# The normalised input of an encoder layer: rows scaled on VectorE and transposed plainly, in place of products with a diagonal

## The chip, the core and the metric

The kernel runs on one core of a Trainium2 chip. Its time is device microseconds of one execution. TensorE does the matmuls and transposes (PE in the rows, PEld is its loading of weights), VectorE (DVE) and ScalarE (ACT) the elementwise work, GpSimd (POOL) small things, and SyncE (SP) issues most transfers.

## The reference

One layer of a hybrid encoder on 256 tokens of width 2048, all in f32: a feed-forward part, a mixing part (attention and convolution), and a second feed-forward part. Each part reads a modulated, normalised input, and its result is normalised and added to x:

```python
def rms_norm(x, g):
    y = xf * lax.rsqrt(jnp.mean(xf * xf, axis=-1, keepdims=True) + NORM_EPS)
    return (y * g.astype(jnp.float32)).astype(x.dtype)

def modulate(h, shift, scale):
    return h * (1.0 + scale[:, None, :]) + shift[:, None, :]
...
        mod = c_act @ w_ada[l] + b_ada[l]
        (sh1, sc1, g1, sh2, sc2, g2, sh3, sc3, g3) = jnp.split(mod, N_MOD, axis=-1)
        h = modulate(rms_norm(x, ffn1_pre_g[l]), sh1, sc1)
        f = swiglu(h, ffn1_w_gate[l], ffn1_w_up[l], ffn1_w_down[l])
        x = x + 0.5 * g1[:, None, :] * rms_norm(f, ffn1_post_g[l])
```

The other two parts begin and end in the same way, with their own gains and modulation vectors.

## The kernel before

x stays on chip as two token tiles of 128 tokens by 2048 (t0 and t1). A product needs its input with the width on partitions, so each part's input is made in 16 K tiles of 128 columns, transposed. `pre_norm` does this two K tiles at a time: a matmul of a 128x128 block of x with a diagonal matrix that holds 1/rms of its tokens (`dg`, made by `diag_of`) transposes and scales it into a PSUM tile `pst` (there are two such places), ACT multiplies by A and adds B (`hf`, line 377; A is (1 + scale) times the gain, B the shift), and `split_to` splits the result into two float32r parts: the high part is a cast on ACT (line 360), the low part a subtraction on VectorE (line 361). All weights are split in the same way (`wchunk`: cast on ACT, subtraction on VectorE, lines 286 and 287), and each product is three matmuls, high by high, high by low and low by high (lines 312 to 314; the moving operand is 512 columns of the weight). The block products with `dg` are plain f32.

`pre_norm` is called at six places. (1) At the start, for K tiles 0 to 3. (2) In the first feed-forward, whose first round of products goes through the 16 K tiles in four stages of four: while the products of a stage run, VectorE sums up the modulation vectors of the next one from transferred pieces of `w_ada` (`mod_sum`, line 190, advanced a little with each weight chunk), TensorE transposes the sums into columns (line 204), ACT copies those (line 209), and then `pre_norm` makes the next stage's K tiles. (3) At the second boundary, between the first feed-forward and the mixing part, for all 16 K tiles, by `next_norm`: residual of t0 (`post_add`, lines 400 to 408), four K tiles of t0, residual of t1, then the rest. (4) At the third boundary, between mixing and second feed-forward, in the same way for four K tiles. (5, 6) In the two later stages of the second feed-forward, six K tiles each.

1/rms comes from `rstd_parts`: the sum of squares is made by ACT (line 335), scaled on VectorE (at the start on ACT), and raised to the power -0.5 on POOL (line 347, tile `r`). `pr` is the same for the part's result before it is added.

The order on each engine is that of a scheduler that follows the program, and each engine takes its instructions strictly in that order.

Of the kernel before, what the change touches and what calls it, by code (L numbers as in the profile page):

```python
# [36 lines left out]
# Chunks over which token tile 0 runs ahead of tile 1 at a part's start and end, and K tiles of  # L37
# tile 0's input that come before the rest.
# [3 lines left out]
# Steps of background work per weight chunk: convolution, modulation in the first feed-forward  # L42
# and in the mixing part.
# [3 lines left out]
# Chunks between an elementwise result and its transposes: rope, activations, conv input.  # L47
# [3 lines left out]
# Buffers for chunks as loaded, and for each of their two parts.  # L51
# [3 lines left out]
# K tiles of the first products of each feed-forward, by stages of their modulation.  # L55
# [5 lines left out]
def encoder_layer(ctx, tc, a, consts, out):  # L61
# [80 lines left out]
    def load_cols(names, i):  # L142
        """Parameter vectors with element j*128+p at [p, j]."""
        rows = work.tile([P, P], F32, tag="rows", name=f"rows{i}")
        at = 0
        for name in names:
            n = a[name].shape[1] // P
            nc.gpsimd.dma_start(rows[at:at + n, :], a[name].rearrange("o (j p) -> (o j) p", p=P))
            pcols[name] = (at, n, i)
            at += n  # L150
        prm = keep.tile([P, sum(a[n].shape[1] for n in names) // P], F32, name=f"prm{i}")
        ps = tr_ps(f"ps_prm{i}")
        nc.tensor.transpose(ps[:, :at], rows[:at, :], ident[:at, :at])
        nc.scalar.copy(prm[:, :at], ps[:, :at])
        pcols[i] = prm
# [12 lines left out]
    def mod_sum(vs, c0, n):  # L168
        """Partial sums over the partitions of columns c0..c0+n of the vectors vs."""
# [26 lines left out]
    def mod_cols(vs, dsts, c0, n):  # L196
        """Columns c0..c0+n of the vectors vs with element j*128+p at dst[p, j]."""
# [17 lines left out]
    def mod_affine(vsh, vsc, gname, A, B, c0, n):  # L215
        """A = (1 + scale) * pre gain, B = shift, for columns c0..c0+n."""
# [9 lines left out]
    def mod_gate(v, gname, factor, gc):  # L226
        """gc = factor * vector v * post gain."""
# [4 lines left out]
    def gate_tile(gc, i):  # L232
        """The column vector gc as a row, the same on every partition."""
# [11 lines left out]
    def slot(tag, shape, name, dt=F32):  # L245
        """A tile of at most SLOT elements in a place that several parts use in turn."""
# [29 lines left out]
    def wchunk(w, r0, kt, cols, name):  # L276
        """K tiles from row r0 on, of 512 columns in equal parts from each of cols on."""
# [12 lines left out]
    class Group:  # L290
        """ps[t] (+)= x[t] @ w over K tiles k0..k0+nk and 512 columns; xT holds the K tiles
        from kx on."""
# [23 lines left out]
    def in_step(work):  # L316
        """Chunks of groups, all of token tile 0 before token tile 1."""
# [7 lines left out]
    def group(*args, head=0, tail=0, **kw):  # L325
        """A group, token tile 0 ahead of tile 1 over the first head and the last tail chunks."""
# [10 lines left out]
    def rstd_parts(ssp, n, name, act=False):  # L337
        """(sum of the columns of ssp / n + EPS) ** -0.5"""
        k = ssp.shape[-1]
        ms, r = small(f"s_{name}", 1), small(name, 1)  # L340
# [9 lines left out]
    def diag_of(r, name, act=False):  # L350
        d = work.tile([P, P], F32, tag="diag", bufs=2, name=name)
        if act:
            nc.scalar.activation(d, ident, AF.Copy, scale=r)
        else:
            nc.vector.tensor_scalar(d, ident, r, None, op0=ALU.mult)
        return d

# [5 lines left out]
    def pre_norm(hT, dg, A, B, j0, j1, i, t0=0, t1=NT):  # L363
        """K tiles j0..j1 of modulate(rms_norm(x)) transposed, for token tiles t0..t1; dg
        holds 1/rms on diagonals."""
        n = (t1 - t0) * P
        for j in range(j0, j1, 2):
            ps = tr_ps(f"pst{i}_{j}_{t0}")
            hf = work.tile([P, 2, S], F32, tag="hf", bufs=2, name=f"hf{i}_{j}_{t0}")
            h = hf[:, :, :n]  # L370
            for jj in range(2):
                o = ps[:, jj * S:jj * S + n]
                for t in range(t0, t1):
                    nc.tensor.matmul(o[:, (t - t0) * P:(t - t0 + 1) * P],  # L374
                                     x[:, t, (j + jj) * P:(j + jj + 1) * P], dg[t],
                                     start=True, stop=True)
# [4 lines left out]
    def transposed(src, ps, n=2):  # L381
        """[P tokens, t, n*128] -> PSUM [128, n, S]."""
# [17 lines left out]
    def post_add(f, r, i, t):  # L400
        """x += f * r for token tile t, r the rstd of the rows before the gain; returns 1/rms
        of the new rows on a diagonal."""
# [5 lines left out]
        return diag_of(rstd_parts(sx, D, f"r{i}_{t}"), f"dg{i}_{t}")  # L408

    def next_norm(f, ssp, A, B, j1, i):  # L410
        """Residual, and the first j1 K tiles of the next part's input, token tile 0 first over
        the chunks of a group's head."""
        hT = Parts(f"h{i}", "h", range(4))
        jh = min(HEAD * CH, j1)
        dg = [post_add(f, post_rstd(ssp, i, 0), i, 0)]
        pre_norm(hT, dg, A, B, 0, JF, i, 0, 1)
        dg.append(post_add(f, post_rstd(ssp, i, 1), i, 1))
        pre_norm(hT, dg, A, B, JF, jh, i, 0, 1)
        pre_norm(hT, dg, A, B, 0, jh, i, 1, 2)
        pre_norm(hT, dg, A, B, jh, j1, i)  # L420
        return hT, dg

# [43 lines left out]
    def ffn_start(hT, wg, wu, i, stages, mods_of, norm_of, last_lane, begin=None):  # L466
        """Blocks of the first round, K tiles in stages: a stage's modulation is summed up
        while the products of the stage before run."""
# [64 lines left out]
    # ================= first feed-forward =================  # L533
# [29 lines left out]
    dg = [diag_of(rstd_parts(sx[t], D, f"r0_{t}", act=True), f"dg0_{t}", act=True) for t in range(NT)]  # L563
# [3 lines left out]
    pre_norm(hT, dg, A1, B1, *STAGES1[0], "1_0")  # L567

    def begin2(open_group, run, order):
        """The first two groups with token tile 0 ahead."""  # L570
# [10 lines left out]
    def later_mods():  # L581
        yield from mod_gate(2, "ffn1_post_g", 0.5, g1)
        for c0 in range(0, D, MW):
# [4 lines left out]
                   lambda s: pre_norm(hT, dg, A1, B1, *STAGES1[s], f"1_{s}"),  # L588
# [4 lines left out]
    hT, dg = next_norm(f, ssp, A2, B2, NK, 2)  # L593

    # ================= attention and convolution =================
# [42 lines left out]
    def rope_T(pt, name, tag):  # L638
        """PSUM t x [P, 4 heads x 128] -> rotated and transposed [128, head, S]."""
# [26 lines left out]
    def attention(hb, qT, kT):  # L666
        """Heads of one half in overlapping steps: scores, transpose, output."""
# [58 lines left out]
    def attn_parts(hb, hi, lo):  # L726
        """Attention rows times their gain, transposed; 1/rms is applied after the product."""
# [30 lines left out]
    # layer norm over channels, swish: sums over channels on the tensor engine  # L758
# [9 lines left out]
    def rstd_cols(ps, n, name):  # L768
        """Sums of [128 equal rows, S tokens] -> 1/rms with the tokens on partitions."""
# [107 lines left out]
    for db in range(4):  # L877
        po = mm_ps(f"pc{db}")
        group(po, mT, w_out, 8, 8, db * BLK, f"oc{db}", kx=8, tail=TAIL if db == 3 else 0)
        for t in range(NT):  # L880
# [4 lines left out]
    # ================= second feed-forward =================  # L885
    hT, dg = next_norm(f, ssp, A3, B3, STAGES2[0][1], 3)
    aT = ffn_start(hT, a["ffn2_w_gate"], a["ffn2_w_up"], 2, STAGES2, ffn2_mods,
                   lambda s: pre_norm(hT, dg, A3, B3, *STAGES2[s], f"3_{s}"),
# [64 lines left out]
```

## Time and profile before

| | |
|---|---|
| time, median of 3 runs | 2000.48 us (1996.08 to 2004.53) |
| span of the profiled execution | 1997.8 us |
| TensorE busy | 1917.2 us (96%) |
| VectorE busy | 1466.7 us (73%) |
| ACT busy | 936.7 us (47%) |
| POOL busy | 65.5 us (3%) |
| transfers | 493.13 MB, mean 247 GB/s |

A busy share is an average over the whole span. Matmuls overlap on TensorE, so the length of one matmul record is longer than the distance to the next. One f32 block product shows as two records in the trace, one plain transpose as one. In the rows, `out<-in` names the tiles by their names in the program, and what stands in brackets is the idle time of the engine ahead of the instruction and what ended it. The granted clock is a share of TensorE's full 2.4 GHz.

### The profile page before, as it was taken

How to read it: one execution, taken by the hardware profiler on the slowest of the kernel's cores; microseconds unless marked ns; L12 is line 12 of the kernel's file. 1: busy time of each engine (PE TensorE's matmuls, PEld its weight loads, DVE VectorE, ACT ScalarE, POOL GpSimd, SP SyncE). 2: the span in 40 equal slices, each digit the busy share in tenths (PEclk: the TensorE clock that was granted, in tenths of full speed). 3: DMA queues.
4: the chain of work that ended last, by engine and by line, in shares of the span. 5: the costliest groups of instructions: out<-in, count | busy, mean ns of one | idle time of the engine just before them, and what ended most of it. 6: DMA issues, size and time to landing. Idle time of an engine off the chain costs nothing.

```text
span 1997.8 us, 23978 instructions
## 1 busy us (share of the span) xinstructions
PE 1917.2 (96%) x8547; PEld 1552.7 (78%) x8547; DVE 1466.7 (73%) x1780; ACT 936.7 (47%) x1439; POOL 65.5 (3%) x90
## 2 busy tenths in 40 slices
PE   2999999999999999899999997999999999999997
PEld 2888888888888877678888786888888777888886
DVE  6789999777777766589997758898776455444454
ACT  3554455444444444644455745635444433444442
POOL 2000000000000000000100000000000000000000
PEclk9999999999999999899999998999999999999999
DMA  9989988999999977356656667998777667656552
GB/s 341 313 296 307 318 266 280 344 320 327 313 318 322 301 251 262 104 176 184 179 167 203 195 205 243 329 325 278 245 224 234 216 231 236 198 180 186 172 189 96
DMA packets 249432, 493.13 MB, mean 247 GB/s; under 512 B 17065, under 2 KB 42433, under 8 KB 249312
## 3 DMA queue, kind: packets, MB, share of 16 engines
q1 hardware_dynamic: 247888, 491.38, 73.8%
q8 instruction: 67, 1.10, 0.2%
q14 instruction: 53, 0.43, 0.1%
q0 software_dynamic: 1248, 0.15, 0.1%
q10 hardware_dynamic: 176, 0.07, 0.0%
HBM read 489.44 MB, written 2.10 MB: 246 GB/s over the span
## 4 chain that ended last, share of the span: by engine, by line
PE 85%; DMA 7%; DVE 4%; issue 2%; ACT 1%; POOL 0%; DVEq 0%; POOLq 0%; ACTq 0%; SPq 0%
PE pg_t L312 8%; PE pg_t L313 8%; PE pg_t L314 8%; PE pu_t L313 8%; PE pu_t L314 7%; PE pu_t L312 7%; DMA ada<-in_w_ada 7%; PE pd_t L313 6%; PE pd_t L314 6%; PE pd_t L312 6%; PE pc_t L312 2%; PE pc_t L313 2%; PE pc_t L314 2%; PE pst L374 1%; DVE lo_d L287 1%
## 5 line engine op out<-in xcount | busy, mean ns | idle before, releaser
L190 DVE SCALAR_TENSOR_TENSOR acc<-ada,cact,acc 128x512 f32<-128x512 f32 (+2 forms) x448 | 394.2, 900 | 148.4 <-DMA ada<-in_w_ada 138.0
L286 ACT CAST hi_d<-raw_d 128x1024 fp32r<-128x1024 f32 x176 | 184.4, 1050 | 273.6 <-PE pd_t L314 233.8
L286 ACT CAST hi_g<-raw_g 128x1024 fp32r<-128x1024 f32 x176 | 184.8, 1051 | 241.4 <-PE pg_t L314 143.8
L287 DVE TENSOR_TENSOR lo_d<-raw_d,hi_d 128x1024 fp32r<-128x1024 f32 x176 | 212.7, 1223 | 111.1 <-ACT hi_d L286 110.7
L286 ACT CAST hi_u<-raw_u 128x1024 fp32r<-128x1024 f32 x176 | 184.7, 1050 | 219.3 <-PE pu_t L314 121.7
L287 DVE TENSOR_TENSOR lo_u<-raw_u,hi_u 128x1024 fp32r<-128x1024 f32 x176 | 214.3, 1223 | 95.9 <-ACT hi_u L286 95.3
L287 DVE TENSOR_TENSOR lo_g<-raw_g,hi_g 128x1024 fp32r<-128x1024 f32 x176 | 214.4, 1223 | 77.1 <-ACT hi_g L286 76.7
L313 PE MATMUL pd_t<-lo_d,a_0h 128*128 128x512 f32 x384 | 152.3, 397 | 4.3 <-DVE lo_d L287 4.2
L312 PE MATMUL pd_t<-hi_d,a_0h 128*128 128x512 f32 x384 | 152.4, 397 | 0.0
L314 PE MATMUL pd_t<-hi_d,a_0l 128*128 128x512 f32 x384 | 151.7, 395 | 0.0
L312 PE MATMUL pg_t<-hi_g,h3h 128*128 128x512 f32 x352 | 141.2, 401 | 1.8 <-ACT h3h L360 1.8
L312 PE MATMUL pg_t<-hi_g,h1h 128*128 128x512 f32 x352 | 140.5, 400 | 0.2 <-ACT h1h L360 0.2
L312 PE MATMUL pu_t<-hi_u,h1h 128*128 128x512 f32 x352 | 140.4, 399 | 0.0
L312 PE MATMUL pu_t<-hi_u,h3h 128*128 128x512 f32 x352 | 140.2, 398 | 0.0
L313 PE MATMUL pg_t<-lo_g,h1h 128*128 128x512 f32 x352 | 139.8, 397 | 0.0
L313 PE MATMUL pg_t<-lo_g,h3h 128*128 128x512 f32 x352 | 139.8, 397 | 0.0
L314 PE MATMUL pg_t<-hi_g,h3l 128*128 128x512 f32 x352 | 139.8, 397 | 0.0
L314 PE MATMUL pg_t<-hi_g,h1l 128*128 128x512 f32 x352 | 139.7, 397 | 0.0
L313 PE MATMUL pu_t<-lo_u,h1h 128*128 128x512 f32 x352 | 139.7, 397 | 0.0
L313 PE MATMUL pu_t<-lo_u,h3h 128*128 128x512 f32 x352 | 139.4, 396 | 0.3 <-DVE lo_u L287 0.3
L314 PE MATMUL pu_t<-hi_u,h3l 128*128 128x512 f32 x352 | 139.4, 396 | 0.0
L314 PE MATMUL pu_t<-hi_u,h1l 128*128 128x512 f32 x352 | 139.2, 396 | 0.0
(258 smaller groups left out, 3631.3 us busy)
## 6 DMA issues: line engine op xcount, KB each, us to landing
ada<-in_w_ada SPq DMA_DIRECT2D x288, 512.0 KB, 5.4
raw_g<-in_ffn_w_gate SPq DMA_DIRECT2D x176, 512.0 KB, 4.9
raw_u<-in_ffn_w_up SPq DMA_DIRECT2D x176, 512.0 KB, 4.9
raw_d<-in_ffn_w_down SPq DMA_DIRECT2D x176, 512.0 KB, 5.3
raw_c<-in_w_in SPq DMA_DIRECT2D x64, 256.0 KB, 3.0
raw_q<-in_w_in SPq DMA_DIRECT2D x16, 512.0 KB, 3.7
raw_k<-in_w_in SPq DMA_DIRECT2D x16, 512.0 KB, 3.7
raw_v<-in_w_in SPq DMA_DIRECT2D x16, 512.0 KB, 3.6
```

The source lines that it names most:

```text
L190: nc.vector.scalar_tensor_tensor(acc, w[:, j, :], cact[:, j0 + j:j0 + j + 1], acc, op0=ALU.mult, op1=ALU.add)
L286: nc.scalar.copy(h, r)
L287: nc.vector.tensor_tensor(l, r, f32(h), op=ALU.subtract)
L312: nc.tensor.matmul(o, xh, h, start=self.first and k == 0, stop=False)
L313: nc.tensor.matmul(o, xh, l, start=False, stop=False)
L314: nc.tensor.matmul(o, xl, h, start=False, stop=self.last and k == self.nk - 1)
L374: nc.tensor.matmul(o[:, (t - t0) * P:(t - t0 + 1) * P], x[:, t, (j + jj) * P:(j + jj + 1) * P], dg[t], start=True, stop=True)
```

## The change

The diagonal goes away. 1/rms itself is kept (`rx`). For each pair of K tiles and each token tile, VectorE writes x times 1/rms into a new tile `xn` of 128x256 (three places), and TensorE transposes its two halves with the identity matrix, as plain transposes. ACT's conversions, the splits and all else stay. Comments are gone as well, so line numbers behind them are lower by some 5: the scaling is line 364, the transposes line 367, the conversions line 372, the cast line 353 and the subtraction line 354.

```diff
-    def diag_of(r, name, act=False):
-        d = work.tile([P, P], F32, tag="diag", bufs=2, name=name)
-        if act:
-            nc.scalar.activation(d, ident, AF.Copy, scale=r)
-        else:
-            nc.vector.tensor_scalar(d, ident, r, None, op0=ALU.mult)
-        return d
...
-    def pre_norm(hT, dg, A, B, j0, j1, i, t0=0, t1=NT):
+    def pre_norm(hT, rs, A, B, j0, j1, i, t0=0, t1=NT):
...
+            for t in range(t0, t1):
+                xn = work.tile([P, 2 * P], F32, tag="xn", bufs=3, name=f"xn{i}_{j}_{t}")
+                nc.vector.tensor_scalar(xn, x[:, t, j * P:(j + 2) * P], rs[t], None, op0=ALU.mult)
+                for jj in range(2):
+                    o = jj * S + (t - t0) * P
+                    nc.tensor.transpose(ps[:, o:o + P], xn[:, jj * P:(jj + 1) * P], ident)
             for jj in range(2):
                 o = ps[:, jj * S:jj * S + n]
-                for t in range(t0, t1):
-                    nc.tensor.matmul(o[:, (t - t0) * P:(t - t0 + 1) * P],
-                                     x[:, t, (j + jj) * P:(j + jj + 1) * P], dg[t],
-                                     start=True, stop=True)
                 nc.scalar.activation(h[:, jj, :], o, AF.Identity,
...
-        return diag_of(rstd_parts(sx, D, f"r{i}_{t}"), f"dg{i}_{t}")
+        return rstd_parts(sx, D, f"r{i}_{t}", keep_in="rx")
...
-    dg = [diag_of(rstd_parts(sx[t], D, f"r0_{t}", act=True), f"dg0_{t}", act=True) for t in range(NT)]
+    rs = [rstd_parts(sx[t], D, f"r0_{t}", act=True, keep_in="rx") for t in range(NT)]
```

The order on the engines shifts too. **The start, VectorE**, where the first modulation sums are accumulated (`acc`, from pieces `ada` of `w_ada`). Before:

```order
L190 SCALAR_TENSOR_TENSOR acc_0_94<-ada_0_6_151,cact,acc_0_94 128x512 x2
L190 SCALAR_TENSOR_TENSOR acc_0_94<-ada_0_6_153,cact,acc_0_94 128x512 x2
L190 SCALAR_TENSOR_TENSOR acc_0_94<-ada_0_8_165,cact,acc_0_94 128x512 x2
L190 SCALAR_TENSOR_TENSOR acc_0_94<-ada_0_8_167,cact,acc_0_94 128x512 x2
L190 SCALAR_TENSOR_TENSOR acc_0_94<-ada_0_10_173,cact,acc_0_94 128x512 x2
```

And with the change:

```order
L190 SCALAR_TENSOR_TENSOR acc_0_94<-ada_0_6_153,cact,acc_0_94 128x512 x2
L364 TENSOR_SCALAR xn_0_0_0_237<-x,r_0_198 128x256
L364 TENSOR_SCALAR xn_0_0_1_241<-x,r_1_203 128x256
L190 SCALAR_TENSOR_TENSOR acc_0_94<-ada_0_8_165,cact,acc_0_94 128x512
L364 TENSOR_SCALAR xn_0_2_0_251<-x,r_0_198 128x256
L190 SCALAR_TENSOR_TENSOR acc_0_94<-ada_0_8_165,cact,acc_0_94 128x512
L190 SCALAR_TENSOR_TENSOR acc_0_94<-ada_0_8_167,cact,acc_0_94 128x512 x2
```

Three scalings, which need `r_0` and `r_1`, now stand inside the accumulation, ahead of its second half.

**The second boundary, TensorE**, behind the last product of the first feed-forward. Before (`pc_t` is the first result of the mixing part, `hi_c` and `lo_c` its weights, `h2h` and `h2l` its input):

```order
L374 MATMUL pst_0_0_6510<-dg_0_6508,x 128x128
L374 MATMUL pst_2_0_6518<-dg_0_6508,x 128x128
L374 MATMUL pst_0_0_6510<-dg_0_6508,x 128x128
L374 MATMUL pst_2_0_6518<-dg_0_6508,x 128x128
L374 MATMUL pst_4_0_6551<-dg_0_6508,x 128x128
L312 MATMUL pc_t_6683<-hi_c_0_6686,h2h_6477 128x512
L313 MATMUL pc_t_6683<-lo_c_0_6687,h2h_6477 128x512
L374 MATMUL pst_6_0_6559<-dg_0_6508,x 128x128
L314 MATMUL pc_t_6683<-hi_c_0_6686,h2l_6478 128x512
```

And with the change:

```order
L367 MATMUL pst_0_0_6536<-ident,xn_0_0_6537 128x128 x2
L367 MATMUL pst_2_0_6546<-ident,xn_2_0_6547 128x128 x2
L312 MATMUL pc_t_6739<-hi_c_0_6742,h2h_6505 128x512
L313 MATMUL pc_t_6739<-lo_c_0_6743,h2h_6505 128x512
L314 MATMUL pc_t_6739<-hi_c_0_6742,h2l_6506 128x512
L312 MATMUL pc_t_6739<-hi_c_0_6742,h2h_6505 128x512
L367 MATMUL pst_4_0_6579<-ident,xn_4_0_6580 128x128 x2
L367 MATMUL pst_6_0_6589<-ident,xn_6_0_6590 128x128 x2
```

The products of the two halves of a PSUM tile stood apart, with those of another tile in between; now the two transposes of a tile are neighbours, and those of K tiles 4 to 7 stand behind four weight matmuls.

**The second boundary, ACT**, from the first conversion on. Before (`jx` are the squares of t1's new x):

```order
L377 ACTIVATE hf_0_0_6511<-pst_0_0_6510,B_89,A_88 128x128
L335 ACTIVATE jx,sx_1_6531<-x 128x512
L377 ACTIVATE hf_2_0_6519<-pst_2_0_6518,B_89,A_88 128x128
L377 ACTIVATE hf_0_0_6511<-pst_0_0_6510,B_89,A_88 128x128
L335 ACTIVATE jx,sx_1_6531<-x 128x512
L360 CAST h2h_6477<-hf_0_0_6511 128x2x128
L377 ACTIVATE hf_2_0_6519<-pst_2_0_6518,B_89,A_88 128x128
```

And with the change:

```order
L372 ACTIVATE hf_0_0_6541<-pst_0_0_6536,B_89,A_88 128x128 x2
L372 ACTIVATE hf_2_0_6551<-pst_2_0_6546,B_89,A_88 128x128
L353 CAST h2h_6505<-hf_0_0_6541 128x2x128
L372 ACTIVATE hf_2_0_6551<-pst_2_0_6546,B_89,A_88 128x128
L335 ACTIVATE jx,sx_1_6561<-x 128x512
L353 CAST h2h_6505<-hf_2_0_6551 128x2x128
```

The first cast, which the first weight product needs, moved ahead of both squares, and the first squares moved behind four conversions.

**The third boundary, VectorE**, from the 1/rms of t0 to the first residual piece of t1. Before:

```order
L346 TENSOR_SCALAR s_r_0_9721<-s_r_0_9721 128x1
L190 SCALAR_TENSOR_TENSOR acc_512_9897<-ada_512_2_9949,cact,acc_512_9897 128x512
L355 TENSOR_SCALAR dg_0_9726<-ident,r_0_9722 128x128
L345 TENSOR_REDUCE s_pr_1_9744<-sspm 128x1
L190 SCALAR_TENSOR_TENSOR acc_512_9897<-ada_512_2_9951,cact,acc_512_9897 128x512
L346 TENSOR_SCALAR s_pr_1_9744<-s_pr_1_9744 128x1
L190 SCALAR_TENSOR_TENSOR acc_512_9897<-ada_512_2_9949,cact,acc_512_9897 128x512
L406 SCALAR_TENSOR_TENSOR x<-fm_8766,pr_1_9745,x 128x512
```

And with the change:

```order
L346 TENSOR_REDUCE s_r_0_9777<-sx_0_9764 128x1
L346 TENSOR_REDUCE s_pr_1_9802<-sspm 128x1
L287 TENSOR_TENSOR lo_u_0_0_0_1_9881<-raw_u_0_0_0_1_9879,hi_u_0_0_0_1_9880 128x1024
L347 TENSOR_SCALAR s_r_0_9777<-s_r_0_9777 128x1
L347 TENSOR_SCALAR s_pr_1_9802<-s_pr_1_9802 128x1
L190 SCALAR_TENSOR_TENSOR acc_512_9957<-ada_512_2_10009,cact,acc_512_9957 128x512
L364 TENSOR_SCALAR xn_0_0_9783<-x,r_0_9778 128x256
L364 TENSOR_SCALAR xn_2_0_9793<-x,r_0_9778 128x256
L401 SCALAR_TENSOR_TENSOR x<-fm_8822,pr_1_9803,x 128x512
```

The sum that the residual of t1 needs (`s_pr_1`) moved ahead of the accumulations and beside that of t0; two scalings stand where the diagonal was.

## Rows read from the trace of the kernel before

**Rows 1.** The page, part 1: busy us (share of the span) and instructions.

```profile
PE 1917.2 (96%) x8547; PEld 1552.7 (78%) x8547; DVE 1466.7 (73%) x1780; ACT 936.7 (47%) x1439; POOL 65.5 (3%) x90
```

**Rows 2.** Stretches: length, busy us of PE, PEld, DVE, ACT, POOL; clock, DMA, GB/s.

```profile
46.00:820.00 774.00, 767.49 (x3419) 621.40 (x3417) 617.40 (x633) 362.23 (x555) 19.30 (x30) 1.00 0.87 298
```

**Rows 3.** Groups by shape: busy us, mean ns | idle us before them.

```profile
L374 PE MATMUL pst<-dg,x 128*128 128x128 f32 x192 | 36.8, 322 | 18.5 <-DVE dg L355 8.2 <-DVE s_pr L346 7.3 <-ACT hf L377 1.3
```

**Rows 4.** Timeline of TensorE: start, us, instruction [idle before <-releaser].

```profile
106.31 1.04 PE L204 MATMUL psc<-ident,acc 128*128 128x128 f32 x8
107.10 0.47 PE L312 MATMUL pu_t<-hi_u,h1h 128*128 128x512 f32 x1
...
111.08 0.97 PEld L374 LDWEIGHTS pst<-dg,x 128*128 128x128 f32 x8 [0.45 <-ACT hf L377]
111.08 1.16 PE L374 MATMUL pst<-dg,x 128*128 128x128 f32 x8
111.99 0.48 PE L313 MATMUL pu_t<-lo_u,h1h 128*128 128x512 f32 x1
```

**Rows 5.** Stretches, line 374 alone: PE, PEld (busy us, records), clock, DMA, GB/s.

```profile
37.00:45.00 8.00, 4.35 (x16) 3.80 (x16) 1.00 1.02 367
109.00:255.00 146.00, 7.97 (x48) 6.31 (x48) 1.00 0.90 306
825.00:852.00 27.00, 13.21 (x64) 10.43 (x64) 0.87 0.24 76
1209.00:1222.00 13.00, 3.67 (x16) 3.03 (x16) 0.67 0.65 204
1280.00:1395.00 115.00, 7.39 (x48) 6.28 (x48) 1.00 0.89 306
```

**Rows 6.** Groups by shape: a scaling on VectorE that exists already.

```profile
L818 DVE TENSOR_SCALAR hfc<-co,prm 128x256 f32<-128x256 f32 x8 | 2.5, 353 | 0.0
```

**Rows 7.** Stretches as in rows 2: a stage of each feed-forward.

```profile
109.50:179.40 69.90, 69.81 (x310) 56.09 (x310) 65.08 (x83) 31.73 (x48) 1.46 (x3) 1.00 0.88 304
...
1284.00:1384.00 100.00, 100.00 (x447) 81.17 (x446) 91.25 (x126) 45.23 (x68) 2.70 (x4) 1.00 0.93 318
```

**Rows 8.** Timeline of all engines, the kernel's start.

```profile
23.66 11.69 DVE L190 SCALAR_TENSOR_TENSOR acc<-ada,cact,acc 128x512 f32<-128x512 f32 x16 [1.17 <-DMA ada<-in_w_ada]
...
25.64 0.40 ACT L353 ACTIVATE dg<-ident,r 128x128 f32<-128x128 f32 x1 [0.37 <-POOL r L347]
...
34.19 1.08 PE L204 MATMUL psc<-ident,acc 128*128 128x128 f32 x4 [19.04 <-DVE acc L190]
...
39.23 0.56 ACT L377 ACTIVATE hf<-pst,B,A 128x256 f32<-128x256 f32 x1
...
41.10 0.56 ACT L377 ACTIVATE hf<-pst,B,A 128x256 f32<-128x256 f32 x1 [0.65 <-PE pst L374]
```

**Rows 9.** Timeline of all engines, second boundary.

```profile
825.32 0.29 DVE L355 TENSOR_SCALAR dg<-ident,r 128x128 f32<-128x128 f32 x1 [0.59 <-POOL r L347]
...
825.66 2.14 PE L374 MATMUL pst<-dg,x 128*128 128x128 f32 x6 [7.26 <-DVE s_pr L346]
...
826.50 0.46 ACT L377 ACTIVATE hf<-pst,B,A 128x128 f32<-128x128 f32 x1 [2.92 <-PE pst L374]
...
827.79 0.79 ACT L377 ACTIVATE hf<-pst,B,A 128x128 f32<-128x128 f32 x2
...
829.53 0.79 PE L312 MATMUL pc_t<-hi_c,h2h 128*128 128x512 f32 x1
```

**Rows 10.** Stretches as in rows 2: second boundary.

```profile
825.60:831.80 6.20, 5.51 (x16) 4.28 (x17) 3.97 (x10) 5.10 (x16) 0.54 (x1) 0.50 0.39 126
834.00:849.00 15.00, 15.00 (x85) 11.80 (x85) 6.76 (x11) 14.01 (x31) 0.00 (x0) 1.00 0.10 29
```

**Rows 11.** Timeline of TensorE, third boundary.

```profile
1213.68 0.80 PE L312 MATMUL pg_t<-hi_g,h3h 128*128 128x512 f32 x1 [1.18 <-ACT h3h L360]
...
1223.06 0.50 PE L312 MATMUL pg_t<-hi_g,h3h 128*128 128x512 f32 x1 [0.60 <-ACT h3h L360]
```

More of the change, by code (lines that the diff above doesn't have):

```diff
@@ L335, in square_sum, with rstd_parts @@
         nc.scalar.activation(junk(name)[:, :src.shape[-1]], src, AF.Square, accum_out=dst)
-    def rstd_parts(ssp, n, name, act=False):
+    def rstd_parts(ssp, n, name, act=False, keep_in=None):
         k = ssp.shape[-1]
-        ms, r = small(f"s_{name}", 1), small(name, 1)
+        ms = small(f"s_{name}", 1)
+        r = work.tile([P, 1], F32, tag=keep_in, bufs=NT, name=name) if keep_in else small(name, 1)
         if act:
@@ L414, in next_norm @@
         jh = min(HEAD * CH, j1)
[L415 to L421, printed above, removed]
+        rs = [post_add(f, post_rstd(ssp, i, 0), i, 0)]
+        pre_norm(hT, rs, A, B, 0, JF, i, 0, 1)
+        rs.append(post_add(f, post_rstd(ssp, i, 1), i, 1))
+        pre_norm(hT, rs, A, B, JF, jh, i, 0, 1)
+        pre_norm(hT, rs, A, B, 0, jh, i, 1, 2)
+        pre_norm(hT, rs, A, B, jh, j1, i)
+        return hT, rs
     def act_out(aT, i, gs, pu, name):
@@ L566, in encoder_layer @@
     hT = Parts("h1", "h", range(4))
-    pre_norm(hT, dg, A1, B1, *STAGES1[0], "1_0")
+    pre_norm(hT, rs, A1, B1, *STAGES1[0], "1_0")
     def begin2(open_group, run, order):
@@ L587, in encoder_layer @@
     aT = ffn_start(hT, a["ffn1_w_gate"], a["ffn1_w_up"], 1, STAGES1, ffn1_mods,
-                   lambda s: pre_norm(hT, dg, A1, B1, *STAGES1[s], f"1_{s}"),
+                   lambda s: pre_norm(hT, rs, A1, B1, *STAGES1[s], f"1_{s}"),
                    (later_mods(), LRATE))
@@ L592, in encoder_layer @@
     drain_all()
-    hT, dg = next_norm(f, ssp, A2, B2, NK, 2)
+    hT, rs = next_norm(f, ssp, A2, B2, NK, 2)
     w_in = a["w_in"]
@@ L883, in encoder_layer @@
             post_block(f, ssp, G2, t, db)
-    hT, dg = next_norm(f, ssp, A3, B3, STAGES2[0][1], 3)
+    hT, rs = next_norm(f, ssp, A3, B3, STAGES2[0][1], 3)
     aT = ffn_start(hT, a["ffn2_w_gate"], a["ffn2_w_up"], 2, STAGES2, ffn2_mods,
-                   lambda s: pre_norm(hT, dg, A3, B3, *STAGES2[s], f"3_{s}"),
+                   lambda s: pre_norm(hT, rs, A3, B3, *STAGES2[s], f"3_{s}"),
                    (mod_gate(8, "ffn2_post_g", 0.5, g3), 0.3), begin2)
```

## The prediction

> **What bounds the kernel now.** I began with the busy shares of the page: TensorE is busy for 96% of the span, all other engines clearly less [rows 1]. The table of stretches shows the same in the longest stretch, 46 to 820 us: 767.5 of 774 us at the full clock [rows 2]. So a matmul taken out of TensorE's row shortens the kernel, unless what is put on VectorE makes TensorE wait. The groups of instructions come next: the products that the change replaces (line 374) are 192 records, and TensorE stood idle for 18.5 us ahead of them [rows 3]. Each full-precision product is two records, so these are 96 blocks of 128x128. The 322 ns of that row are latency and not a price, as matmuls overlap. The price is the distance to the next start. In the timeline eight records of line 374 begin at 111.08 and the next product at 111.99: 0.91 us, or 0.228 us for a block. Just before, eight plain transposes of line 204, the same instruction that the change uses, begin at 106.31 and the next product at 107.10: 0.79 us, 0.099 us for a block [rows 4]. A block thus saves 0.129 us at the full clock, if TensorE is the bound where it stands; 96 of them would save 12.4 us.
>
> By place [rows 5] the records are 16 in the kernel's start, 48 in the first feed-forward's stages, 64 at the second boundary, 16 at the third, and 48 in the second feed-forward's stages: 8, 24, 32, 8 and 24 blocks. The places have different bounds, so each has its own term.
>
> **The added work.** 48 scalings of 128x256 elements go on VectorE. The same operation in the same shape exists already, at 353 ns [rows 6]: 48 x 0.353 = 16.9 us, against four diagonals taken away (1.1 us in all, at the 0.29 us that the one at 825.32 took [rows 9]). VectorE is not the bound overall (73% [rows 1]), but in a stage of the first feed-forward it is busy for 65.1 of 69.9 us [rows 7]. Four scalings there are 1.4 us, and 4.8 us are idle.
>
> **Stages of the feed-forwards.** First: TensorE is busy 69.81 of 69.90 us in a stage [rows 7], so its work counts in full: 24 x 0.129 = 3.1 us. VectorE's order puts the scalings of a stage early, except the fourth, which waits for one of three buffers, so only that one can be late. Bounds: 0 (VectorE with its 1.4 us becomes the bound) and 4.1 (also 1 us of the pauses in which TensorE waits for ACT between the halves of a tile, such as the 0.45 us at 111.08 [rows 4], as both halves are now transposed together). I take 3.1, since the 4.8 us of idle time cover 1.4. Second: the stage shows TensorE at 100 of 100 us and VectorE at 91 [rows 7], again 24 blocks, 3.1 us, bounds 1.5 and 3.6.
>
> **The kernel's start.** In VectorE's order three scalings now stand inside the accumulation of the modulation sums. They need 1/rms, which ACT saw at 25.64 for the second token tile (its dg there waited for POOL), while VectorE ran accumulations back to back from 23.66 [rows 8]. By the order one of these comes ahead of the scalings, so VectorE is free at about 24.4. It waits for both values until 25.64, ends the second scaling at 26.0, and does a third: 26.0 - 24.4 + 0.35 = 2.0 us later for the rest of the accumulation. TensorE's first transposes wait for that accumulation (34.19, [rows 8]), so this is a loss on the path. Given back: the two conversions of a tile stood at 39.23 and 41.10, since the second one's products had to wait for the first; now only 0.56 us separates them, 1.3 us sooner. The last four records go away from behind the first product at half clock, about 0.7 us. Sum 0; bounds a loss of 2 and a gain of 1.
>
> **The second boundary** (residual, then the input of the mixing part; 32 blocks). At the front, products began at 825.66, ACT converted the first half at 826.50, the second at 827.79 and the first weight product came at 829.53 [rows 9]. Now two scalings (0.71 us) stand where a diagonal did (0.29), both halves arrive together, and in ACT's order two halves, one more and the cast stand ahead of the first sum of squares: hf, hf, hf, cast from 826.5 at some 0.4 us each, product near 828.1, 1.4 us sooner. After that TensorE would save 26 x 0.129 = 3.3 us, but from 834 to 849 ACT is busy 14.0 of 15.0 us [rows 10], with the same conversions and casts as now. There it allows 1.0 us. I take 1.4 + 1.0 = **2.4**. Bounds: 0.5 (the later residual of token tile 1, 0.4 us behind the scalings, keeps most) and 4.7 (1.4 + 3.3, ACT no limit).
>
> **The third boundary** (8 blocks). The same front, 1.4 us sooner, and 4 later blocks (0.5 us). But token tile 1 comes through residual, sum of squares and POOL, and its first product waited 0.60 us already [rows 11]. A sooner tile 0 then waits longer for tile 1, if that doesn't move. In VectorE's order its residual no longer stands behind three accumulations, so it moves too, by less. I take 1.2, bounds -0.5 and 2.5.
>
> **Sum.** 3.1 + 3.1 + 0 + 2.4 + 1.2 = 9.8 us. The profiled execution's span is 1997.8 us, 2.7 below the median of the three timed runs (which lie within 1996.1 to 2004.5). I expect a span of 1988.0 and a median of 2000.5 - 9.8 = **1990.7 us**. With the likelier bounds of each term the forecast has a range of its own of 1986 to 1996.
>
> **A rule that speaks against it.** The row of line 204 gives 0.099 us for a transpose that follows others, though each record lasts about 0.27 us. The Trainium skill ("TensorE: Matmul & The Clock Gate", section Part 4: PE-mode transpose) gives some 275 ns for a transpose of this size in a kernel and says that the higher clock does not engage for transposes. By 275 ns the 96 transposes would be 26.4 us against 21.9 now, a loss of 4.5. The trace does not agree on the distance; on the clock no stretch of it has transposes alone, so both are rivals below.
>
> **Rivals.**
> *ACT and VectorE give it back.* The 2.0 us at the start stay lost, the first feed-forward's gain goes to VectorE's 1.4 us a stage (0), the second boundary is paced by ACT (1.5), the third by token tile 1 (0.5), the second feed-forward keeps 2.8: 2.8 us, **1997.7**. For it: 93% in [rows 7] and ACT in [rows 10]. Against it: the idle time in these rows.
> *More than the products.* The pauses between halves go too: start +1, feed-forwards 4.1 and 3.6, second boundary 4.7, third 2: 15.4 us, **1985.1**. For it: the 18.5 us of idle time in [rows 3]. Against it: most of those are the two long waits for a residual, which stay.
> *A clock that stays low: slower.* After its pause at the second boundary TensorE ran at 0.50 of its clock (1.2 GHz) until 831.8, with products of line 374 from 825.66 on [rows 9, 10]. If transposes do less for the clock than those products, weight products go on at the lower level. If the some 19 us until 851 stayed there, 43 products at 0.20 us more (310 matmuls in 69.9 us [rows 7] are 0.23 us each at the full level; at half near twice that) and 26 transposes at 0.1 more are 11 us; 25 more products at the third boundary are 5. 16 - 9.8 = 6 us slower, **2006.7**. It decides from a loss of 9.8 us, some 49 products at half clock. Against it: dense 128x512 products follow within 2 us of the transposes.
> *Transposes at their latency: slower.* Where each pair waits for its own scaling, a transpose could cost its 0.27 us. 96 x 0.27 = 25.9 against 21.9 loses 4.0 us in place of gaining 12.4; with 1.4 sooner at the boundary and the 2 us at the start, **2005**. It decides above 0.228 us for a transpose. Against it: scalings stand well ahead of the transposes in the stages.
>
> **How the numbers follow.** Forecast 0.52, give-back 0.24, more 0.13, clock 0.06, latency 0.05. Faster or slower by 0.5% (10 us, about what a measurement of this kernel can tell from no change) is decided right at the forecast's centre: a little under half of it and nearly all of "more" give faster 0.37; half of the slower cases with their tails give slower 0.07, the rest, with the give-back, same 0.56. 1983 to 2002 holds the forecast, the give-back and most of "more", and leaves out the slower two and the end of "more", together 2 in 10.
>
> **What would show it.** Right: 96 records of transposes with the next start some 0.1 us on; stages of the first feed-forward about 1 us shorter each, with VectorE near 95% and no wait of TensorE for a scaling; the first weight product at the second boundary within 3 us of the first transpose; TensorE's first transposes near 36 us in place of 34.2. Wrong: TensorE waiting for line 364 inside the stages, weight products of the boundaries still at half clock long after the first, or stages as long as before.

## The result, and the profile after

The changed kernel takes 1969.3 us (median of 4 runs, 1965.4 to 1970.8), the kernel before, run beside it, 2001.7. The ratio is 0.9844, with an interval of 0.9830 to 0.9858: 1.6% faster. The forecast was 1990.7 us and the range ended at 1983. The mechanism that was forecast is there, but it is a third of the gain; the rest came from a place that the forecast didn't look at.

The page of the changed kernel, part 1:

```profile
PE 1881.0 (96%) x8451; PEld 1534.9 (78%) x8451; DVE 1474.6 (75%) x1824; ACT 932.5 (47%) x1437; POOL 64.1 (3%) x90
```
VectorE is 8 us busier and TensorE 36 us less [rows 1], though the price of the blocks fell by only 12 us: 96 products at 0.228 us are 21.9, 96 transposes at the 0.103 us read below are 9.9. The groups by shape show the new operations:

```profile
L367 PE MATMUL pst<-ident,xn 128*128 128x128 f32 x96 | 17.8, 313 | 19.4 <-DVE xn L364 16.1 <-ACT hf L372 1.7 <-ACT jc L209 1.3
...
L364 DVE TENSOR_SCALAR xn<-x,r 128x256 f32<-128x256 f32 x48 | 15.6, 351 | 7.5 <-PE pst L367 3.2 <-POOL r L348 2.3 <-DMA ada<-in_w_ada 1.6
```
There are 96 records of transposes in place of 192 [rows 3], and 48 scalings at 351 ns, the price that was taken from [rows 6]. The distance between transposes is in TensorE's timeline of the same stage as [rows 4]:

```profile
108.66 0.66 PE L367 MATMUL pst<-ident,xn 128*128 128x128 f32 x4
109.07 0.47 PE L312 MATMUL pu_t<-hi_u,h1h 128*128 128x512 f32 x1
```
Four of them in 0.41 us are 0.103 us each, against 0.099 forecast. In the table of all waits there is one row of TensorE for a scaling; its columns are us in total, times, longest:

```profile
PE pst L367 <- DVE xn L364: 16.1, 2, 8.7
```
These are the two boundaries, where the wait for the residual's 1/rms stood before. So no stage waits for a scaling on VectorE. The stretches that answer to [rows 7] and [rows 10], with the columns of [rows 2]:

```profile
107.50:176.50 69.00, 68.84 (x308) 55.76 (x306) 66.62 (x87) 32.69 (x55) 2.38 (x5) 1.00 0.92 313
811.00:818.00 7.00, 5.88 (x18) 4.18 (x17) 4.03 (x11) 5.70 (x18) 0.00 (x0) 0.50 0.31 100
820.00:834.50 14.50, 14.50 (x73) 10.53 (x71) 10.23 (x21) 14.18 (x31) 0.00 (x0) 1.00 0.23 71
1254.00:1355.00 101.00, 101.00 (x455) 82.59 (x454) 96.22 (x141) 48.03 (x74) 3.35 (x5) 1.00 0.95 326
```
VectorE is at 97% of a stage of the first feed-forward (66.62 of 69.00) and at 95% of one of the second (96.22 of 101.00) without holding TensorE up. At the second boundary ACT is at 14.18 of 14.50 us, fuller than before. These stretches don't begin and end at the same products as those before, so they don't tell what a stage gained. Two starts of the same product do, with one stage's 8 blocks between them, before:

```profile
117.87 0.39 PE L312 MATMUL pg_t<-hi_g,h1h 128*128 128x512 f32 x1
...
187.78 0.39 PE L312 MATMUL pg_t<-hi_g,h1h 128*128 128x512 f32 x1
```
and after:

```profile
116.12 0.39 PE L312 MATMUL pg_t<-hi_g,h1h 128*128 128x512 f32 x1
...
183.57 0.39 PE L312 MATMUL pg_t<-hi_g,h1h 128*128 128x512 f32 x1
```
That is 69.91 us before and 67.45 after, 2.46 less, where the blocks were to save 1.03. The timeline of the second boundary:

```profile
810.28 0.63 DVE L364 TENSOR_SCALAR xn<-x,r 128x256 f32<-128x256 f32 x2 [0.60 <-POOL r L348]
...
810.69 1.11 PE L367 MATMUL pst<-ident,xn 128*128 128x128 f32 x4 [7.35 <-DVE xn L364]
...
811.42 1.16 ACT L372 ACTIVATE hf<-pst,B,A 128x128 f32<-128x128 f32 x3 [2.88 <-PE pst L367]
...
812.92 0.80 PE L312 MATMUL pc_t<-hi_c,h2h 128*128 128x512 f32 x1 [1.12 <-ACT h2h L353]
```
From the first transpose to the first weight product it is 2.23 us; with the diagonal it was 3.87 [rows 9]. The third boundary:

```profile
1193.05 0.79 PE L312 MATMUL pg_t<-hi_g,h3h 128*128 128x512 f32 x1 [1.11 <-ACT h3h L353]
...
1202.01 0.51 PE L312 MATMUL pg_t<-hi_g,h3h 128*128 128x512 f32 x1 [0.85 <-ACT h3h L353]
```
The wait of the second token tile's first product grew from 0.60 to 0.85 us [rows 11], as the forecast had it for a sooner first tile. And the start:

```profile
24.30 0.35 DVE L364 TENSOR_SCALAR xn<-x,r 128x256 f32<-128x256 f32 x1 [1.60 <-DMA ada<-in_w_ada]
24.82 0.35 DVE L364 TENSOR_SCALAR xn<-x,r 128x256 f32<-128x256 f32 x1 [0.17 <-POOL r L348]
...
25.75 0.35 DVE L364 TENSOR_SCALAR xn<-x,r 128x256 f32<-128x256 f32 x1
...
35.76 1.09 PE L204 MATMUL psc<-ident,acc 128*128 128x128 f32 x4 [20.75 <-DVE acc L190]
...
40.81 0.56 ACT L372 ACTIVATE hf<-pst,B,A 128x256 f32<-128x256 f32 x1
...
41.52 0.57 ACT L372 ACTIVATE hf<-pst,B,A 128x256 f32<-128x256 f32 x1
...
42.14 1.11 PE L367 MATMUL pst<-ident,xn 128*128 128x128 f32 x4 [1.66 <-ACT hf L372]
...
43.44 0.79 PE L312 MATMUL pg_t<-hi_g,h1h 128*128 128x512 f32 x1
```
The scalings stand in the accumulation, as the order said. The first begins after 1.60 us of idle time, where an accumulation began after 1.17 before, and the transposes of the sums begin at 35.76 in place of 34.19 [rows 8].

All this doesn't make 32 us. Two starts of the same products in both kernels show the rest. Here are, in the kernel before, the first product of one block of the first down projection and of the next:

```profile
397.15 0.40 PE L312 MATMUL pd_t<-hi_d,a_0h 128*128 128x512 f32 x1
...
430.64 0.39 PE L312 MATMUL pd_t<-hi_d,a_0h 128*128 128x512 f32 x1
```
Between these stand 144 weight products and nothing of the change: 33.49 us. The same two in the changed kernel, and two starts of the gate projection with 192 products between:

```profile
390.81 0.40 PE L312 MATMUL pd_t<-hi_d,a_0h 128*128 128x512 f32 x1
...
423.88 0.40 PE L312 MATMUL pd_t<-hi_d,a_0h 128*128 128x512 f32 x1
...
501.80 0.39 PE L312 MATMUL pg_t<-hi_g,h1h 128*128 128x512 f32 x1
...
547.92 0.39 PE L312 MATMUL pg_t<-hi_g,h1h 128*128 128x512 f32 x1
```
The 144 products now take 33.07 us. Over all records of the two traces, the mean distance between the starts of neighbouring weight products (at the full clock, where nothing stands between and nothing is waited for) is 232.7 ns before and 229.2 ns after, in every part of the kernel. There are 7680 of them: 26.5 us, of which 1.0 falls on the 285 products of the stage above. That is the term that was missing.

### The profile page after: what moved, and what is told of

Read it like the earlier page. It is cut to its first block, busy times and chain, and to the rows that moved or that the text cites. A ratio compares the mean times of both kernels' runs of the same rounds, so it can differ in the third digit from the quotient of the medians.

```text
span 1968.4 us, 23857 instructions
## 1 busy us (share of the span) xinstructions
PE 1881.0 (96%) x8451; PEld 1534.9 (78%) x8451; DVE 1474.6 (75%) x1824; ACT 932.5 (47%) x1437; POOL 64.1 (3%) x90
## 4 chain that ended last, share of the span: by engine, by line
PE 79%; DMA 10%; DVE 6%; issue 2%; ACT 2%; POOL 0%; SPq 0%; DVEq 0%; POOLq 0%; ACTq 0%
DMA ada<-in_w_ada 8%; PE pg_t L312 8%; PE pg_t L313 8%; PE pg_t L314 8%; PE pu_t L314 7%; PE pu_t L312 7%; PE pu_t L313 7%; PE pd_t L313 6%; PE pd_t L314 6%; PE pd_t L312 6%; PE pc_t L312 2%; PE pc_t L314 2%; PE pc_t L313 2%; DVE acc L190 2%; DVE lo_d L287 2%
## 5 line engine op out<-in xcount | busy, mean ns | idle before, releaser
L286 ACT CAST hi_g<-raw_g 128x1024 fp32r<-128x1024 f32 x176 | 185.0, 1052 | 232.3 <-PE pg_t L314 129.6
```

The lines of the kernel that those rows point to most:

```text
L286: nc.scalar.copy(h, r)
```

## The experiments

Ratios are to the kernel before, run beside each group of kernels: 2001.7 us beside the changed kernel, 1991.7 to 1992.5 beside the experiments. Times of the first group and of the others therefore don't compare.

**Where the operands lie.** In the program as placed, the diagonals left (2 tiles of 512 bytes per partition), the kept 1/rms came (2 of 32), and the three `xn` tiles (1024 each) stand behind the transposed input `h`, ahead of the activations `a`. (The traces hold no addresses: these come from the program, and the distances below are their test.) So `h` moved by -1024 + 64 = -960 bytes and `a` by -960 + 3072 = 2112, both by 64 more than a multiple of 256. `h` and `a` are the stationary operands of the weight products, the weight parts `hi` and `lo` the moving ones, and those didn't move. From `hi` to `h` or `a` it was 128 more than a multiple of 256 before, and is 192 after. The first four runs shift tiles by unused bytes: behind the diagonals or `rx` (e1 and e2), ahead of the weight tiles (e4), and at both places (e3).

```diff
+    pad = work.tile([P, 16], F32, tag="pad", name="pad")        # e1, e2, e3
+    nc.gpsimd.memset(pad, 0.0)
     hT = Parts("h1", "h", range(4))
...
+    pad0 = keep.tile([P, 16], F32, name="pad0")                 # e3, e4
+    nc.gpsimd.memset(pad0, 0.0)
     ident = keep.tile([P, P], F32, name="ident")
```

> The kernel before, unchanged but for 64 unused bytes per partition that shift all work tiles behind the diagonals, the transposed input (h) and the activations (a) among them, from a remainder of 64 to one of 0 in 128 bytes, as they lie in the changed kernel; the weights' parts stay at 64. Theory A (the distance between the products depends on where the stationary operand lies): products stand some 229 ns apart instead of 232.7, and with 7680 of them the time falls by about 25 us, to some 1976. Rival B (the closer products come from the changed order or the removed diagonals themselves): no change, some 2001.

> The changed kernel with the same 64 unused bytes, which put h, a and the tiles behind them back to a remainder of 64 in 128 bytes, as before the change. Theory A: products 232.7 ns apart again, time up by about 25 us, to some 1995, which would leave some 6 us for the change's own work. Rival B: no change, some 1969.

> The changed kernel with 64 unused bytes ahead of the weight tiles and 64 behind the kept 1/rms: weight parts (moving operand), h and a (stationary) all at a remainder of 0 in 128 bytes. Theory A, stationary operand alone: as the changed kernel, some 1969, or sooner if the moving operand's place counts too. Rival C (what counts is that the two operands lie differently within 128 bytes): slow, some 1995, since both have the same remainder as before the change.

> The changed kernel with 64 unused bytes ahead of the weight tiles alone: weight parts at a remainder of 0, h and a at 64, the other way round than in the changed kernel. Theory A: slow, some 1995, as the stationary operand is at 64. Rival C: fast, some 1969, as the two lie differently. Rival B: 1969.

| run | from moving to stationary operand, remainder in 256 | distance | us | ratio, interval |
|---|---|---|---|---|
| before | 128 | 232.7 ns | 2001.7, 1991.7 | 1 |
| after | 192 | 229.2 | 1969.3 | 0.9844, 0.9830 to 0.9858 |
| e1 (before, shifted) | 192 | 229.2 | 1971.6 | 0.9896, 0.9882 to 0.9911 |
| e2 (after, shifted) | 0 | 227.3 | 1950.8 | 0.9797, 0.9782 to 0.9811 |
| e3 (after, both at 0) | 0 | 227.3 | 1948.0 | 0.9779, 0.9764 to 0.9793 |
| e4 (after, weights at 0) | 192 | 229.3 | 1960.6 | 0.9844, 0.9827 to 0.9860 |

Rival B fell at once: e1 has the old order and the old products, and 64 unused bytes alone make it 1.0% faster. Its block of 144 products takes 33.07 us, as in the changed kernel:

```profile
393.86 0.40 PE L312 MATMUL pd_t<-hi_d,a_0h 128*128 128x512 f32 x1
...
426.92 0.40 PE L312 MATMUL pd_t<-hi_d,a_0h 128*128 128x512 f32 x1
```
But theory A fell too: e2 should have lost the gain and was quicker than the changed kernel, and e4, with `h` and `a` at another alignment, was like it. Rival C fell with e3, which it had slow. What kernels with one distance share is the difference of the two operands' places. The same block of 144 products in e2:

```profile
387.28 0.39 PE L312 MATMUL pd_t<-hi_d,a_0h 128*128 128x512 f32 x1
...
420.03 0.39 PE L312 MATMUL pd_t<-hi_d,a_0h 128*128 128x512 f32 x1
```
32.76 us. From this came theory D, that the difference of the places decides, and the next four runs: `pad` of 128 bytes in the kernel before (e5), of 128 and 256 in the changed one (e6, e7), and 64 bytes between `hi` and `lo` (e8).

> The kernel before, unchanged but for 128 unused bytes behind the diagonals, so that the stationary tiles (h, a) lie a multiple of 1024 bytes behind the weight parts. Theory D (the distance between products depends on the address of the stationary operand less that of the moving one: 232.7 ns at -128, 229.2 at -64, 227.3 at 0): products 227.3 ns apart, about 30 us less than before, ratio near 0.985. The change's own work is then the difference between this and the changed kernel in the same place (0.9797): some 0.5%, 10 us. Rival B (the changed order brings the close products): ratio as in the first shifted run, 0.99, or 1.

> The changed kernel with 128 unused bytes: the stationary tiles 64 bytes past the multiple of 1024, at the remainder of 0 in 128 that the changed kernel has on the other side. Theory D, if only the distance from 0 counts: 229 ns, ratio as the changed kernel, 0.984; if it is not symmetrical another level, but uniform over the kernel. Theory A (alignment to 128 bytes): as the changed kernel exactly.

> The changed kernel with 256 unused bytes: the stationary tiles 192 bytes past the multiple. Theory D with a level that grows with the distance from 0: 234 ns or more apart, some 35 us slower than at 0, ratio near 1. If the levels repeat every 256 bytes: 229.2, as at -64.

> The changed kernel with 64 unused bytes between the high and the low parts of the weights: against the stationary tiles the high parts lie at 0 and the low parts at -64. Theory D: in one kernel, the start after a product that streams a high part comes 227.3 ns on, after one that streams a low part (line 313's) 229.2 ns on or somewhat more, ratio between 0.980 and 0.984. Rival E (VectorE's and ACT's traffic meets the products): the same distances after high and low parts.

| run | remainder | distance | us | ratio, interval |
|---|---|---|---|---|
| e5 (before) | 0 | 227.3 ns | 1964.3 | 0.9868, 0.9853 to 0.9882 |
| e6 (after) | 64 | 233.4 | 1985.7 | 0.9971, 0.9961 to 0.9982 |
| e7 (after) | 192 | 229.2 | 1961.0 | 0.9851, 0.9836 to 0.9866 |
| e8 (after) | `hi` 0, `lo` 192 | 231.8, 232.0 | 1978.3 | 0.9938, 0.9923 to 0.9953 |

e5 and e2 agree, e7 repeats the changed kernel, so the levels repeat every 256 bytes; and they are not symmetrical (64: 233.4, 192: 229.2). The last activation tile's low part lies 32 bytes off the others in all these kernels, and the some 127 starts ahead of its products give four levels more in the same traces: 232.0 at 32, 234.0 at 96, 231.2 at 160, 234.4 at 224. e8 contradicts the rule in the form that it was given: products that stream a high part were expected at 227.3 ns, and all were at some 232, alike behind both parts, as rival E had it. So one pair of operands doesn't decide alone; the kernels at 227.3 ns are those where all three agree.

That it is not the other engines' traffic (rival E) is supported by the traces: before, the distance is 232.7 ns at 1865 starts with VectorE and ACT both busy throughout, 232.3 at 324 starts with both idle; after, 229.1 and 229.8. With transfers it is the same: before, 232.8 ns at 546 starts with no packet under way, 232.7 at 3952 with 14 or more of them; after, 229.5 and 229.2. Two runs settle it: unused bytes between `h` and `a` (e13, the `pad` one line further down, behind the `h` tiles), and 256 bytes between `hi` and `lo` (e14).

> The changed kernel with 64 unused bytes between the transposed input (h, still at -64 against the weight parts) and all work tiles behind it, the activations (a) among them (now at 0). If the distance between products is set by the two operands that TensorE itself reads: in one kernel, products that read h (gate, up and input projections) 229.2 ns apart, products that read a (down projections) 227.3. If it is set by the kernel's layout as a whole or by other engines' traffic: the same distance for both.

> The changed kernel at 0 with the low parts of the weights moved by 256 bytes against the high parts, h and a still at a multiple of 256 against both. Levels repeat every 256 bytes and all three operands agree: 227.3 ns, ratio 0.98. If it was the distance of exactly 16384 bytes between high and low parts that counted when 64 bytes between them slowed all products to 231.9 ns: slower, some 232 ns, ratio 0.994.

The same starts in e13, down projection (reads `a`) and gate projection (reads `h`):

```profile
391.09 0.39 PE L312 MATMUL pd_t<-hi_d,a_0h 128*128 128x512 f32 x1
...
423.85 0.39 PE L312 MATMUL pd_t<-hi_d,a_0h 128*128 128x512 f32 x1
...
501.43 0.39 PE L312 MATMUL pg_t<-hi_g,h1h 128*128 128x512 f32 x1
...
547.54 0.39 PE L312 MATMUL pg_t<-hi_g,h1h 128*128 128x512 f32 x1
```
32.76 us for 144 products with `a` at 0, as in e2; 46.11 us for 192 with `h` at 192, as in the changed kernel (46.12; e2 has 45.77 there). Both levels stand in one kernel, by operand: 227.4 and 229.3 ns. Ratio 0.9848 (0.9824 to 0.9872). e14 has 227.3 ns and 0.9783 (0.9764 to 0.9803): 256 bytes between `hi` and `lo` change nothing, where 64 did.

**The change without the shift.** With the operands at the same remainder, the kernels before and after are e1 and e4 (192): 0.9896 and 0.9844, 0.53%, 11 us; and e5 and e2 (0): 0.9868 and 0.9797, 0.7%, 13 us. Product by product, e5 and e2 differ by steps and by nothing in between, so that each place of the change can be read off; e11 and e12 divide it further. e11 has plain transposes in the old order of halves, e12 the full-precision products with both halves ahead of the conversions:

```diff
             for jj in range(2):                                  # e12
                 o = ps[:, jj * S:jj * S + n]
                 for t in range(t0, t1):
                     nc.tensor.matmul(o[:, (t - t0) * P:(t - t0 + 1) * P],
                                      x[:, t, (j + jj) * P:(j + jj + 1) * P], dg[t],
                                      start=True, stop=True)
+            for jj in range(2):
+                o = ps[:, jj * S:jj * S + n]
                 nc.scalar.activation(h[:, jj, :], o, AF.Identity,
...
             for jj in range(2):                                  # e11
                 o = ps[:, jj * S:jj * S + n]
+                for t in range(t0, t1):
+                    nc.tensor.transpose(o[:, (t - t0) * P:(t - t0 + 1) * P],
+                                        xn[t][:, jj * P:(jj + 1) * P], ident)
                 nc.scalar.activation(h[:, jj, :], o, AF.Identity,
```

> The changed kernel at 0, with plain transposes, but in the order of the kernel before: a tile's first half, its conversion, then the second half. If the plain transpose's lower price is all of the gain, as the prediction had it: no change, 0.9797. If the neighbouring halves are worth a part of their own (the measured gain by place is 14 us where the prices give 9.8): some 4 us slower, 0.982, lost at the stages of the feed-forwards and the boundaries.

> The kernel before at 0, with full-precision products and the diagonal, but both halves of a tile issued ahead of their two conversions. The same question from the other side: if the halves' order is worth some 4 us, 1960, ratio 0.985 against 0.9868; if only the price counts, no change.

Gain against e5 in us, from the starts of the same products in one profiled execution of each:

| place | forecast | e2 (the change) | e11 (plain, halves apart) | e12 (full, halves together) |
|---|---|---|---|---|
| start | 0 | -2.5 | -2.9 | -2.1 |
| stages of the first feed-forward | 3.1 | 0.95, 1.3, 3.2 | 0.8, 1.2, 2.9 | 0.1, 0.25, 2.3 |
| behind them (305 to 335 us) | | -0.6 | -4.7 | -0.6 |
| 700 to 770 us | | 4.1 | -0.5 | 0.1 |
| second boundary | 2.4 | 4.9 | 4.3 | 1.3 |
| mixing part | | 1.2 | 0.1 | -0.5 |
| third boundary | 1.2 | 2.6 | 0.9 | 1.35 |
| stages of the second feed-forward | 3.1 | 1.6, 1.8 | 1.6, 1.6 | 0.6, 0.3 |
| 1520 to 1680 us | | -4.6 | 0.1 | 4.7 |
| ratio to before | | 0.9797 | 0.9855, 0.9835 to 0.9874 | 0.9843, 0.9823 to 0.9862 |

The steps at 305, 700 and 1520 us are no places of the change. At 1520 two kernels that differ by a common shift alone (e2 and e3) drift by 4.6 us against each other too, so that step can't be put down to the change; at 700 TensorE waited for the low parts of weights, in e5

```profile
PE pd_t L313 <- DVE lo_d L287: 3.8, 2, 2.0
```
and in e2

```profile
PE pd_t L313 <- DVE lo_d L287: 0.7, 1, 0.7
```
Why that wait is shorter in e2 wasn't tried. The halves' order is worth little in most stages (plain transposes: 0.1 to 0.3 us a stage) and 1.7 at the third boundary. The third step of the first feed-forward is special: in e5 TensorE stood for 2.0 us in that stage (246 to 256 us) behind a conversion, which e11 and e12 are rid of as well:

```profile
PE pst L374 <- ACT hf L377: 2.0, 1, 2.0
```
e12 came as expected for an order worth some 4 us (1959.8 us, 0.9843), but in its trace 4.7 of its 7.7 us stand at 1520 us; at the places of the change its gains sum to 4.1, those of e11 to 10.4. So the price alone gives about the 9.8 us that were forecast, and the order 4, with the pause of 2.0 us in both. e11's expectation was missed: it lost some 11 us against e2, not 4. At the places of the change it is 3.6; 4.1 more went at 305 us and 4.6 at 700, where no halves stand, and at 1520 it lost 4.7 less. Whether the losses at 305 and 700 come of its order or of this one execution isn't shown. In 306 to 332 us the transposes of activations wait for a copy of modulation sums:

```profile
PE pa L381 <- ACT jc L209: 3.3, 1, 3.3
```
And behind that wait TensorE ran at half clock (the column ahead of the last two):

```profile
324.80:328.10 3.30, 3.30 (x9) 2.56 (x8) 2.80 (x3) 1.10 (x5) 0.00 (x0) 0.50 0.75 252
```
**The start.** e10 is e2 with the four scalings of the start on ACT; e9 has that, and the last activation tile lengthened by 32 bytes, so that all operands agree.

```diff
+                if act:
+                    nc.scalar.activation(xn, x[:, t, j * P:(j + 2) * P], AF.Copy, scale=rs[t])
+                else:
                     nc.vector.tensor_scalar(xn, x[:, t, j * P:(j + 2) * P], rs[t], None, op0=ALU.mult)
...
-SLOT = 4 * (S + 2 * PAD)
+SLOT = 4 * (S + 2 * PAD) + 8
```

> The changed kernel at 0, with the four scalings of the kernel's start on ACT, nothing else. If the scalings inside VectorE's accumulation are what made the first products 2.5 us later than in the kernel before at 0, the first products come back by about 2 us or more and everything behind them keeps that: ratio some 0.9785 against 0.9797. If not (transposes wait for something else): first products as late as before, 0.9797.

> The changed kernel with its stationary tiles at 0 against the weight parts (64 unused bytes), the scalings of the kernel's start on ACT in place of VectorE, and the last activation tile lengthened by 32 bytes, so that its low part lies at 0 too (in the runs so far it was at -32, where the products stand 234.4 ns apart, 128 of them: 0.9 us). Start 2.4 us back, last tile 0.9: ratio some 0.978, the fastest of all.

e10 is at 0.9778 (0.9755 to 0.9800). Its products are 1.26 us sooner than e2's from the start on, not 2. The rest of the accumulation, in e5, e10 and e2 in turn:

```profile
22.32 11.69 DVE L190 SCALAR_TENSOR_TENSOR acc<-ada,cact,acc 128x512 f32<-128x512 f32 x16 [1.13 <-DMA ada<-in_w_ada]
23.55 11.69 DVE L190 SCALAR_TENSOR_TENSOR acc<-ada,cact,acc 128x512 f32<-128x512 f32 x16 [1.18 <-DMA ada<-in_w_ada]
25.60 10.90 DVE L190 SCALAR_TENSOR_TENSOR acc<-ada,cact,acc 128x512 f32<-128x512 f32 x15
```
It ends at 34.01, 35.24 and 36.50 us. Part of that is when the pieces of `w_ada` landed: the 16th accumulation began at 20.44 us in e5, at 21.61 in e10 and at 21.23 in e2. From its start to the end of the 32nd it is 13.4 to 13.6 us in the six kernels without scalings there and 14.9 to 15.3 in the other ten. So the scalings cost 1.3 to 1.8 us; of the 2.5 us between e5 and e2, 1.7 are theirs and 0.8 is the landing. Against e5 the landing is in the whole row "start" of the table (0.3 us in e11, 1.1 in e12). e9 measured 1947.4 us, 0.9778 (0.9761 to 0.9795): the fastest of all with e10 and e3, 2.2% faster than the kernel before. Its start came 0.8 us back, not 2.4; the starts ahead of the last tile's low part are 226.7 ns apart, where e2 has 234.4, which makes about the 0.9 us that was expected.

## Why the prediction was wrong

**What failed.** The sum had terms for the places where blocks are replaced and none for the weight products. Their distance was read from the stage ("310 matmuls in 69.9 us are 0.23 us each") and taken as a constant. It is not one: it follows where the tiles lie, and the change moved them by way of `rx` and `xn`. e1 measures that alone: 1.04% of the 1.56%, some 20 us. By the distances it would be 26.5, and the trace of e1 is in fact 26 us shorter than that of the kernel before; but that trace was taken in the group where the kernel before ran 10 us slower. What the remaining 6 us are isn't shown. Longer waits for the low parts of the weights of the down projections are not seen in e1. The row of all such waits (us in total, times, longest), before:

```profile
PE pd_t L313 <- DVE lo_d L287: 8.7, 7, 2.7
```
and in e1:

```profile
PE pd_t L313 <- DVE lo_d L287: 4.4, 5, 2.5
```
**What held.** The price of a block: 0.103 us a transpose. With it the stages of the second feed-forward gain 3.3 us where 3.1 was said, and two of the first's 0.95 and 1.3 where 8 blocks by 0.129 are 1.03. VectorE's 1.4 us a stage lie in its idle time: no product waited for them. The sum of 9.8 us measured 11 and 13 at equal places.

**Sizes that were off.** The first feed-forward's third stage held a pause of 2.0 us; the bound of 4.1 had only 1 us for such pauses. The second boundary's 2.4 was 4.9: the front gave 1.65 us (said: 1.4), and the limit by ACT was set too tight. From the first conversion to the last cast it went from 23.5 us (e5) to 21.6 (e2); I had counted the 1.0 us of ACT's idle time from 834 to 849 and left out its idle time ahead of that, while it waits for 1/rms of the second token tile. Some 0.7 of the 4.9 is clock, and not the change's: behind its first product e5 ran 4.6 us at half clock, e2 3.1, and that time varies as much between kernels of one kind (below). The start's 0 was a loss of some 1.7 from the scalings (said: 2.0) and no gain against it (said: 2.0): the first weight product stands behind the second pair's transposes now, and these waited 1.66 us for a conversion.

**The rivals.** Give-back occurred at the start alone. Latency did not occur: the transposes' records last 0.27 us, but they follow each other 0.103 us apart. "More than the products" was right in its direction and wrong in its cause. The low clock was not the end either. At the second boundary the products of the changed kernel stayed at half clock until 818.3 us, 5.3 us behind the first of them, where it was 2.4 in the kernel before. But that pair is no sign of the transposes: with the full-precision products e1, e12 and e5 stayed 3.8, 4.2 and 4.6 us, and the other kernels with transposes 3.1 to 6.3.

## What to carry to other kernels

Where a change adds, drops or resizes a tile, compare where the operands of the costliest matmuls lie before and after, and look at the distance between matmuls in a part that the change doesn't touch: a shift there is worth more than many an edit, and padding tests it in one run. Where a kernel is bound by its matmuls, try the remainder in 256 bytes of all their operands first, since it is free: here 1.3% for the kernel before (e5), and 1.7% between two places in the changed one (e6 and e2). And price two kernels by their steps at equal places; the median mixes the edit with what it moves.

## What the runs showed of the hardware

Products of 128x128 by 128x512 float32r at the full clock stood 227.3 to 234.4 ns apart, by the difference of the addresses of stationary and moving operand, as its remainder in 256 bytes. Four levels come from whole kernels, over 7200 starts in each: 227.3 at 0, 233.4 at 64, 232.7 at 128, 229.2 at 192. Four come from the some 127 starts ahead of the last tile's products alone: 232.0 at 32, 234.0 at 96, 231.2 at 160, 234.4 at 224. The levels at 0 and 192 are the same within 0.2 ns in kernels of different order; 64 and 128 have one kernel each. It matters little whether VectorE, ACT or transfers are busy (0.7 ns at most, in the traces before and after). Two moving operands that differ by 64 bytes took even the one that agreed to 232. Why the places count, no run here shows.

A plain f32 transpose of 128x128 stood 0.099 to 0.103 us from the next start, a full-precision product of the same size 0.228.
